# Four edits to a two-layer decoder kernel: kept output blocks in another order, half-width products beside each other, a second queue for weights, one O two steps later

## The chip, the cores and the metric

The kernel runs on one NeuronCore of a Trainium2 chip. A core has five engines that work side by side, each with a queue of its own that it goes through in order: TensorE (PE in the profile, with its weight loads as PEld), VectorE (DVE), ScalarE (ACT), GpSimd (POOL) and SyncE (SP). SyncE issues most of the transfers between device memory and the on-chip memory SBUF; GpSimd issues some. TensorE writes to a small memory, PSUM, in banks of 512 float32 columns. The metric is the device time of one execution in microseconds (us).

## The reference

Two residual layers over 1024 tokens of width 1024, then a last RMS norm.

```python
def reference(x, ...):
    for i in range(DEPTH):                       # DEPTH = 2
        h = rms_norm(x, norm_g[i])
        if i % N_MIXERS == 0:
            x = x + lru_mixer(h, ...)            # gated linear recurrence, width 1536
        else:
            x = x + fox_mixer(h, ...)            # 16 heads of 64, causal, with forget gates
    return rms_norm(x, final_g)

def fox_mixer(h, w_in, b_f, w_out):
    u = h @ w_in                                 # q, k, v, gate, f_logit
    cum = jnp.cumsum(jax.nn.log_sigmoid(f_logit + b_f), axis=1)
    logits = q @ k.T * scale + (cum_q - cum_k)   # causal mask
    o = softmax(logits) @ v
    y = o * jax.nn.silu(gate)
    return y @ w_out
```

## The kernel before

**Numbers in two parts.** Nearly all products are made three times: each float32 operand is split into a high part (`to_hi`, a rounding copy) and a low part (`to_lo`, what is left), and TensorE adds high x high, low x high and high x low (`gemm_steps`). Weights come from device memory in pieces of 128 x 512 (`split_weights`, `weights`, lines 111 to 126): `fetch` (line 56) issues the load on the queue that `loads_by` names, SyncE's; `wf` is the landing buffer (3 of them), `wh` and `wl` the two parts (4 each); ScalarE makes the high part, VectorE or GpSimd the low one.

**Stages.** Tokens are two halves of 512. First the recurrent layer (lines 184 to 531, up to about 440 us of the profile): for each of 12 blocks `product`, `conv`, `gates`, `silu`, `recur`, `outputs`, and `project_out` for pairs of blocks. `square_x` and `norm_row` make the first norm: eight squared blocks a half, seven of which are added into one tile, then two products with ones. The last square of each half lies in the fourth of four slots (`sq[3]`), which the other half's squares use too. `softplus` prepares the decay constants with small instructions. At the end of that layer x is stored to device memory (`x1d`), and `squares` and `inv_rms` make the next norm out of column sums: for every 128 tokens one product of a tile of sums with a column of ones, and one more for the last square, which is kept apart (`wait`, line 520).

Then the attention layer (lines 538 to 1127). Of a head `hd` of 16:

- `maxima(hd, c)` (line 762) goes through the four 128-row tiles of a half `c`: scores `S` in PSUM (two buffers), row maximum on VectorE, exponential on ScalarE, division by the sum (line 799 splits off the high part on ScalarE, line 800 the low part on VectorE, both float16 in `both`), and a transposing transfer on SyncE's queue into `turned_` (tile name pT).
- `weigh(hd, c)` (line 808) makes `O`: for each of 4 (first half) or 8 (second half) blocks `j` of keys, v's high and low columns (64 + 64) times the high and the low part of the turned weights, so 8 or 16 products into one PSUM bank. ScalarE (line 829) and VectorE (line 830) add the two 64-row halves of the bank into `yo`. `gated` (line 833) multiplies by the gate `sgs[pair]` after the second head of a pair.
- `kq_units`, `g_units`, `values` project the keys, queries, gates and values of later heads. `values(g)` serves four heads; it is made at the heads 3, 7 and 11 for the next four, from weights in four pieces (k = 0, 2, 4, 6), of which two are loaded before the run below, and the rest after it.

**Order.** `run(order, ...)` (line 853) takes a string: a digit takes the next step of that generator, a point the next step of `fill`, which is 6 products of other work. In a head `first` runs `weigh(hd, 0)` and `maxima(hd, 1)`, `second` runs `weigh(hd, 1)` and `maxima(hd + 1, 0)`; the strings are in lines 29 to 32 (`LAST` from head 12). TensorE's order is held by `tc.issue_after(pe[0].ins)`, which queues what is traced in its block behind the named instruction on the same engine, without waiting for it to end. Where nothing pins it, the order on each engine comes from a scheduler that runs when the program is built.

**The last heads.** From head 12 the fill is the output projection over the first six pairs of heads: `partial` (line 912) makes 16 blocks (8 blocks `db` of 128 outputs, both halves) of 18 products each. A block's x is fetched from `x1d` by GpSimd's queue, the product is added to it on VectorE (line 924), and it is stored again by GpSimd (line 926). It goes through a ring `R` of two buffers, except for four blocks of the first half that are kept in SBUF at a `home` (line 902): block 3 in a tile with the tag `sg`, shared with the gates `sgs` of the last pairs, and 5, 6 and 7 in a tile with the tag `T0`, the keys of the even heads. At the end `turned` (line 957) transposes the sums, adds the last two pairs' product and scales; `residual` (line 932) fetches the first half's other four blocks (0, 1, 2, 4) again.

## Time and profile before

| what | us |
|---|---|
| median of 3 runs (1078.75 to 1080.11) | 1079.31 |
| the profiled execution | 1079.6 |
| its span, first to last instruction | 1077.8 |
| TensorE busy | 1048.0 |
| VectorE busy | 782.1 |
| ScalarE busy | 621.6 |
| GpSimd busy | 113.2 |

The profile is of one execution. A row of the timeline has the start and the length in us, the engine, the line, the operation, and the tiles that it writes and reads; what stands in brackets is how long the engine had been idle, and what ended that. The line is that of the helper that issues the instruction (L60 for nearly all products), so one tells them apart by their tiles: `ops` for blocks of `partial`, `gps` for the projections, `vps` for values, `S` and `O` as above, `fps` for the transposes of the forget gates. Rows that end a wait by VectorE's name may stand for a transfer or another instruction of the same release; the time then tells which.

### The profile page before, as it was taken

Reading aid. Unit: us, or ns where it says so; the run is one execution under the profiler, and the core shown is the slowest. Engines: PE = TensorE matmul, PEld = TensorE weight load, DVE = VectorE, ACT = ScalarE, POOL = GpSimd, SP = SyncE. Lnnn points to the kernel's source line nnn. Section 1 sums busy time; section 2 is a strip of 40 time slices with the busy share of each in tenths; the row PEclk is TensorE's granted clock in tenths of the full one; section 3 lists DMA queues with packets and bytes.
Section 4 is the critical chain, followed back from the end, with each engine's and each line's share of the span. In section 5 each row is a group of like instructions: output and inputs, shape, how many; then the busy total and the mean of one; then the engine's idle time right before and its main releaser. Section 6 shows DMA issues by size and latency. Waiting matters only on the chain. (4 is left out here: it accounts for less than half of the span.)

```text
span 1077.8 us, 14962 instructions
## 1 busy us (share of the span) xinstructions
PE 1048.0 (97%) x5100; PEld 843.7 (78%) x5100; DVE 782.1 (73%) x1444; ACT 621.6 (58%) x1082; POOL 113.2 (11%) x91
## 2 busy tenths in 40 slices
PE   9999999999999999999999999999999999997997
PEld 7788888888888887797777797767977779765776
DVE  7889657766776589947878848788488866774665
ACT  8488453655465564745757636566466655653454
POOL 1322021202220210030000000000000000011200
PEclk9999999999999999999999999999999999998999
DMA  7111211222122112535878957899578885988994
GB/s 251 60 43 50 64 59 54 64 69 64 54 70 68 49 54 69 158 94 134 157 174 192 176 135 155 179 190 191 139 153 188 174 191 131 226 210 225 224 193 157
DMA packets 218508, 142.55 MB, mean 132 GB/s; under 512 B 161792, under 2 KB 178688, under 8 KB 218432
## 3 DMA queue, kind: packets, MB, share of 16 engines
q1 hardware_dynamic: 216032, 133.74, 52.3%
q0 software_dynamic: 2400, 7.87, 2.4%
q8 instruction: 40, 0.66, 0.3%
q14 instruction: 36, 0.29, 0.1%
HBM read 63.82 MB, written 14.81 MB: 73 GB/s over the span
## 5 line engine op out<-in xcount | busy, mean ns | idle before, releaser
L60 PE MATMUL gps<-hh,wh 128*128 128x512 f32 x576 | 227.3, 395 | 0.0
L60 PE MATMUL gps<-hh,wl 128*128 128x512 f32 x576 | 226.4, 393 | 0.8 <-DVE wl L101 0.7
L60 PE MATMUL gps<-hl,wh 128*128 128x512 f32 x576 | 226.6, 393 | 0.0
L90 ACT CAST wh<-wf 128x512 fp32r<-128x512 f32 (+2 forms) x162 | 97.3, 605 | 113.5 <-PE ops L60 43.0
L791 ACT ACTIVATE p<-S,m 128x128 f32<-128x128 f32 (+7 forms) x128 | 94.7, 740 | 67.6 <-DVE m L786 37.9
L101 POOL TENSOR_TENSOR wl<-wf,wh 128x512 fp32r<-128x512 f32 (+1 forms) x50 | 91.9, 1850 | 369.9 <-ACT wh L90 358.3
L60 PEld LDWEIGHTS gps<-hl,wh 128*128 128x128 f32 x576 | 108.4, 188 | 25.0 <-issue 0.5
L60 PEld LDWEIGHTS gps<-hh,wl 128*128 128x128 f32 x576 | 108.6, 189 | 22.5 <-DVE wl L101 1.0
L60 PEld LDWEIGHTS gps<-hh,wh 128*128 128x128 f32 x576 | 108.5, 188 | 21.6
L800 DVE SCALAR_TENSOR_TENSOR pp<-p,sums,pp 128x128 f16<-128x128 f32 (+7 forms) x128 | 103.1, 814 | 19.1 <-ACT pp L92 17.9
L92 ACT ACTIVATE pp<-p,sums 128x128 f16<-128x128 f32 (+7 forms) x128 | 95.5, 770 | 31.2 <-DVE sums L798 15.6
L786 DVE CUSTOM_DVE_ANT_0 S<-S,mask 128x128 f32<-128x128 f32 (+7 forms) x128 | 97.2, 760 | 16.9 <-PE S L60 15.6
L60 PE MATMUL S<-T,U 96*128 96x512 f32 (+7 forms) x384 | 94.3, 355 | 8.1 <-ACT p L791 8.0
L101 DVE TENSOR_TENSOR wl<-wf,wh 128x512 fp32r<-128x512 f32 x112 | 74.4, 668 | 25.8 <-ACT wh L90 25.6
L60 PEld LDWEIGHTS S<-T,U 128*128 128x128 f32 (+1 forms) x384 | 67.9, 190 | 26.2 <-ACT p L791 14.3
L389 DVE TENSOR_TENSOR x<-x,ops 128x512 f32<-128x512 f32 x80 | 54.1, 683 | 41.5 <-PE ops L60 41.4
L60 PE MATMUL ups<-hh,wh 128*128 128x512 f32 x192 | 75.6, 395 | 1.2 <-ACT hh L92 1.2
L60 PE MATMUL ups<-hl,wh 128*128 128x512 f32 x192 | 76.6, 399 | 0.2
L60 PE MATMUL ops<-yh,wl 128*128 128x512 f32 x192 | 75.7, 394 | 0.9 <-DVE wl L101 0.9
L60 PE MATMUL ops<-yh,wh 128*128 128x512 f32 x192 | 75.8, 396 | 0.5 <-DVE x L513 0.5
L60 PE MATMUL ups<-hh,wl 128*128 128x512 f32 x192 | 75.8, 395 | 0.0
L60 PE MATMUL O<-pT,v 128*128 128x512 f16 (+3 forms) x396 | 71.3, 322 | 3.8 <-DMA pT<-pp 3.6
(188 smaller groups left out, 1985.8 us busy)
## 6 DMA issues: line engine op xcount, KB each, us to landing
wf<-in_w SPq DMA_DIRECT2D x106, 256.0 KB
wf<-in_wo SPq DMA_DIRECT2D x64, 128.0 KB
T<-qkh SPq DMA_DIRECT2D x64, 128.0 KB
U<-qkh SPq DMA_DIRECT2D x64, 128.0 KB
x<-in_xt SPq DMA_DIRECT2D x16, 256.0 KB
wvf<-in_wv SPq DMA_DIRECT2D x32, 128.0 KB
x1d<-x SPq DMA_DIRECT2D x16, 256.0 KB
wf<-in_wv SPq DMA_DIRECT2D x16, 256.0 KB
```

Of the source, the lines that this page charges most:

```text
L60: pe[0] = nc.tensor.matmul(*args, **kw)
L90: nc.scalar.copy(hi, src)
L92: nc.scalar.activation(hi, src, AF.Copy, scale=scale)
L101: return eng.tensor_tensor(lo, src, f32(hi), ALU.subtract)
L389: nc.vector.tensor_tensor(x, x, pt, ALU.add)
L786: nc.vector.tensor_tensor_reduce(S[:, :n], S[:, :n], mask[:, SEQ - n :], -1.0, -NEG, ALU.add, ALU.min, accum_out=m)
L791: seen[0] = nc.scalar.activation(p, S[:, :n], AF.Exp, bias=m, scale=-1.0, accum_out=sums[:, i : i + 1])
L800: nc.vector.scalar_tensor_tensor(both[:, :, 1], p, r, both[:, :, 0], ALU.mult, ALU.subtract)
```

## The change

Four edits, and small ones with them.

- **Kept blocks.** The blocks of the first half that stay in SBUF are 4, 5, 6, 7 instead of 3, 5, 6, 7. Block 4 is the one in the tile with the tag `sg`, whose other half is later block 3's; the tile `T0` holds 2, 5, 6, 7. `residual` fetches 0 to 3 again.
- **Low products.** In `weigh(hd, 1)` over a whole half, the low part of the turned weights meets v's high columns alone (the product low x low is left out). Each such product has 64 columns of the array, and writes rows 0 to 63 or 64 to 127 of the bank; they follow in pairs, one for each half of the array. The steps that `run` sees stay four.
- **Values' last weights.** At heads 3, 7 and 11 the pieces k = 4 and 6 are loaded by GpSimd's queue, and are issued before the last maxima tile of `second` instead of after the run. O's copies on ScalarE (line 829) are queued behind the last of those casts, and in every head but the last, for the second half, behind the last split of line 799.
- **Head 14's last O.** `second` of head 14 has its first O two points later.
- In the first norm the last square has a slot of its own, the square roots go behind the squares of both halves, and `softplus` behind the taps of `conv(0)`. In the second, the second half's last square is added on VectorE like the others.

```diff
     pe = [None]
     loads_by = [nc.sync]
+    loaded_last, cast_last = [None], [None]
     def fetch(to, src):
-        loads_by[0].dma_start(to, src)
+        loaded_last[0] = loads_by[0].dma_start(to, src)
     def matmul(*args, **kw):
...
         if eng is nc.scalar:
             if scale is None:
-                nc.scalar.copy(hi, src)
+                cast_last[0] = nc.scalar.copy(hi, src)
             else:
                 nc.scalar.activation(hi, src, AF.Copy, scale=scale)
...
         acc = long("m2")
         sq = [z[:, cs] for z in (long("th"), long("ti")) for cs in halves]
+        sq_ = long("sg")
+
+        squared = [None]
         def square_x(h):
...
             sums[h].append(to)
             for k in range(KT):
-                z = sq[k % 4] if k else to
-                nc.scalar.activation(z, xs[h][k], AF.Square)
+                z = sq_[:, halves[h]] if k == KT - 1 else sq[k % 4] if k else to
+                squared[0] = nc.scalar.activation(z, xs[h][k], AF.Square)
                 if k == KT - 1:
                     sums[h].append(z)
...
             row = ps.tile([P, HALF], F32, tag="O", name="rsrow")
-            for i, sq_ in enumerate(sums[h]):
-                matmul(row, onesf, sq_, start=i == 0, stop=i == len(sums[h]) - 1)
+            for i, z in enumerate(sums[h]):
+                matmul(row, onesf, z, start=i == 0, stop=i == len(sums[h]) - 1)
             r_ = rs[:, halves[h]]
-            nc.scalar.activation(r_, row, AF.Sqrt, bias=epst, scale=1.0 / SEQ)
-            return nc.vector.reciprocal(r_, r_)
+            with tc.issue_after(squared[0].ins):
+                nc.scalar.activation(r_, row, AF.Sqrt, bias=epst, scale=1.0 / SEQ)
+            nc.vector.reciprocal(r_, r_)
         for _ in zip(split_x(0), square_x(0)):
...
                 for _ in zip(split_x(1), square_x(1)):
                     pass
-                done = norm_row(0)
+                norm_row(0)
             else:
                 gates(n - 1)
...
                 product(gps[:, 1], 1, first[1])
                 norm_row(1)
-                with tc.issue_after(done.ins):
+            conv(n, both)
+            if n == 0:
+                with tc.issue_after(state[0]["tap"].ins):
                     softplus()
-            conv(n, both)
             if n % 2 and n > 1:
                 fill = itertools.chain(fill, project_out((n - 3) // 2))
...
                         x,
                         lambda: nrm.tile([P, HALF], F32, tag="sq" if db else "ss", name="sq", bufs=2),
-                        wait=db == KT - 1,
+                        wait=h == 0 and db == KT - 1,
                     )
             rms_row(sums, rs1[h], rms1[h])
...
                 if ex:
                     src.append((wf[:, k : k + 2], slice(256, 256 + ex)))
+                loads_by[0] = nc.gpsimd if k > 3 and not ex else nc.sync
                 parts += split_weights(src, (2, 256 + ex), nc.scalar, nc.gpsimd if ex else nc.vector)
-                if k == 2:
+                loads_by[0] = nc.sync
+                if k == 2 or k == 6 and not ex:
                     yield
             Vs[2 * g], Vs[2 * g + 1] = [], []
...
         stats, pT = {}, {}
+        split_last = [None]
+
+        def after(i):
+            return tc.issue_after(behind[i].ins) if behind else nullcontext()
+
         def maxima(hd, c):
...
                 nc.vector.tensor_scalar(r, r, 1.0 / TOP, None, ALU.mult)
                 nc.vector.reciprocal(r, r)
-                to_hi(both[:, :, 0], p, nc.scalar, scale=r)
+                split_last[0] = nc.scalar.activation(both[:, :, 0], p, AF.Copy, scale=r)
                 nc.vector.scalar_tensor_tensor(both[:, :, 1], p, r, both[:, :, 0], ALU.mult, ALU.subtract)
                 turns.append(
...
             O = ps.tile([P, HALF], F32, tag="O", name="O")[:, : end - begin]
             nj = end // P
+            beside = c == 1 and sub.stop - sub.start == HALF
             for j in range(nj):
                 v = V[j][:, 2 * s : 2 * s + 2].rearrange("p a d -> p (a d)")
                 q = max(begin, j * P)
-                for t in range(2):
+                for t in range(1 if beside else 2):
                     p = turned_[:, j, t, q - c * HALF : end - c * HALF]
-                    matmul(O[:, q - begin :], v, p, start=j == t == 0, stop=j == nj - 1 and t == 1)
-                if j % 2 and j < nj - 1:
+                    matmul(O[:, q - begin :], v, p, start=j == t == 0, stop=not beside and j == nj - 1 and t == 1)
+                if j % 2 and j < nj - 1 and (j % 4 == 3 or not beside):
                     yield
+            if beside:
+                yield
+                for j, a in ((0, 0), (1, 1), (2, 0), (3, 1), (4, 0), (5, 1), (6, 1), (7, 0)):
+                    q = max(begin, j * P)
+                    matmul(
+                        O[a * HD : (a + 1) * HD, q - begin :],
+                        V[j][:, 3 * s],
+                        turned_[:, j, 1, q - c * HALF : end - c * HALF],
+                        start=False,
+                        stop=j > 5,
+                    )
+                    if j == 3:
+                        yield
             r0, r1 = s * HD, (1 - s) * HD
             to, one = yo[r0 : r0 + HD], unit_v[:, hd // 4 : hd // 4 + 1]
-            nc.scalar.activation(to, O[r1 : r1 + HD], AF.Copy, scale=one[r1 : r1 + HD])
+            with after(1), tc.issue_after(split_last[0].ins) if c and hd < HEADS - 1 else nullcontext():
+                nc.scalar.activation(to, O[r1 : r1 + HD], AF.Copy, scale=one[r1 : r1 + HD])
             nc.vector.scalar_tensor_tensor(to, O[r0 : r0 + HD], one[r0 : r0 + HD], to, ALU.mult, ALU.add)
             yield
...
         seen = [None]
-        def run(order, *gens, fill=iter(()), side=iter(())):
-
-            for i in order:
+        behind = []
+
+        def run(order, *gens, fill=iter(()), side=iter(()), vals=None):
+
+            for n, i in enumerate(order):
+                if vals and n == order.rfind("1"):
+                    next(vals)
+                    behind[:] = loaded_last[0], cast_last[0]
                 with tc.issue_after(pe[0].ins):
                     next(fill if i == "." else gens[int(i)], None)
...
         def home(db):
-            if db == 3:
+            if db == 4:
                 two = at.tile([P, 2, HALF], F32, tag="sg", name="x3")
-                homes[3], homes[2] = two[:, 0], two[:, 1]
+                homes[4], homes[3] = two[:, 0], two[:, 1]
             elif db == 5:
                 four = tu.tile([P, 4, HALF], F32, tag="T0", name="x4")
-                homes.update((4 + i, four[:, i]) for i in range(4))
+                homes.update(zip((2, 5, 6, 7), (four[:, i] for i in range(4))))
             return homes[db]
...
                     split_out(db + 1)
-                kept = c == 0 and db in (3, 5, 6, 7)
+                kept = c == 0 and db > 3
                 x = home(db) if kept else rpool.tile([P, HALF], F32, tag="R", name="xp")
                 nc.gpsimd.dma_start(x, x1d[c, :, db])
...
                 two = tu.tile([P, 2, HALF], F32, tag="U0", name="x0")
                 homes[0], homes[1] = two[:, 0], two[:, 1]
-                for d in (0, 1, 2, 4):
+                for d in range(4):
                     fetch(homes[d], x1d[c, :, d])
             if c == 0:
...
                 fill = chain(g_units(pair + 1), kq_units(pair + 2, ((1, (0,)),)))
             first, second = LAST if hd > 11 else ORDER
+            if hd == HEADS - 2:
+                second = "1.1..1..1....0.0.00"
             if hd == HEADS - 1:
                 first = "1..1.0.1.0.1..."
...
             if hd == 14:
                 side = chain(side, late())
+            vals = None
             if hd % 4 == 3 and hd < 12:
-
                 vals = values(hd // 4 + 1)
                 next(vals)
-            run(second, weigh(hd, 1), maxima(hd + 1, 0), fill=fill, side=side)
+            run(second, weigh(hd, 1), maxima(hd + 1, 0), fill=fill, side=side, vals=vals)
+            behind.clear()
             drain(side)
             gated(hd, 1)
...
             if hd < 12:
                 drain(fill)
-            if hd % 4 == 3 and hd < 12:
+            if vals:
                 drain(vals)
         quarters = [slice(0, 256), slice(256, HALF)]
         gated(15, 0)
```

2 lines of the change are left out of this document (1 added, 1 removed).

## The prediction

> **What bounds the kernel now.** I read first the page's busy times, then the stages, then TensorE's waits.
>
> ```profile
> PE 1048.0 (97%) x5100; PEld 843.7 (78%) x5100; DVE 782.1 (73%) x1444; ACT 621.6 (58%) x1082; POOL 113.2 (11%) x91
> ...
> 0.00:440.00 440.00, 436.09 (x1872) 351.97 (x1873) 328.45 (x373) 256.74 (x369) 86.58 (x52) 1.00 0.23 73
> 440.00:506.00 66.00, 65.28 (x390) 57.29 (x389) 45.53 (x98) 37.86 (x66) 10.32 (x9) 1.00 0.46 125
> 506.00:930.00 424.00, 413.67 (x2203) 332.94 (x2202) 315.11 (x772) 254.05 (x499) 0.00 (x0) 1.00 0.79 168
> 930.00:1000.00 70.00, 62.57 (x272) 46.75 (x271) 45.84 (x99) 34.61 (x64) 10.92 (x20) 0.95 0.92 233
> 1000.00:1040.00 40.00, 39.20 (x189) 29.97 (x189) 27.29 (x64) 19.54 (x37) 4.91 (x10) 1.00 1.05 218
> 1040.00:1077.80 37.80, 31.16 (x184) 24.82 (x182) 19.90 (x43) 18.81 (x49) 0.51 (x1) 0.96 0.50 160
> ...
> PE S L60 <- ACT p L791: 8.0, 9, 2.1
> PE ops L60 <- DVE sums L797: 5.5, 1, 5.5
> PE O L60 <- DMA pT<-pp: 3.6, 5, 1.4
> ```
>
> The stage rows give start and end, length, then the busy time of PE, PEld, DVE, ACT and POOL, PE's granted clock, the share of the DMA engines and GB/s. TensorE is busy 97% of the span and at full clock everywhere but in 930 to 1000, where 7.4 us of 70 are idle and the clock falls to 0.95, and in the tail after 1040, which the change does not touch. So a change pays in two ways: fewer columns through TensorE, or less idle time in that one stage. Over the rest of the heads' part (506 to 930) DVE has work for 315 of 424 us and ACT for 254, so neither has to become the bound when TensorE is a few per cent quicker. The first 440 us hold 4 us of idle time in all: nothing that is moved there can win more.
>
> **The order of kept blocks.** The 5.5 us wait is one event, at 985 us. First VectorE's queue, then GpSimd's, then TensorE's, then two pieces of the chain:
>
> ```profile
> 984.40 0.69 DVE L839 TENSOR_TENSOR yo<-yo,sg 128x512 f32<-128x512 f32 x1
> ...
> 986.31 0.89 DVE L800 SCALAR_TENSOR_TENSOR pp<-p,sums,pp 128x640 f16<-128x640 f32 x1
> 990.13 0.69 DVE L924 TENSOR_TENSOR x<-x,ops 128x512 f32<-128x512 f32 x1 [2.93 <-DMA x<-x1d]
> ...
> 974.54 0.54 POOL L921 DMA_DIRECT2D xp<-x1d  x1 [3.56 <-DMA x1d<-xp]
> ...
> 981.32 0.54 POOL L921 DMA_DIRECT2D xp<-x1d  x1 [4.13 <-DMA x1d<-xp]
> 985.38 0.54 POOL L921 DMA_DIRECT2D x<-x1d  x1 [3.53 <-DVE sums L798]
> 992.37 0.55 POOL L926 DMA_DIRECT2D x1d<-xp  x1 [6.45 <-DVE sums L798]
> ...
> 984.27 1.08 PE L60 MATMUL S<-T,U 128*128 128x512 f32 x4 [0.31 <-ACT p L791]
> 990.87 0.80 PE L60 MATMUL ops<-yhh,wh 128*128 128x512 f32 x1 [5.52 <-DVE sums L797]
> 991.47 0.63 PE L60 MATMUL ops<-yhh,wl 128*128 128x512 f32 x1
> ...
> 990.89 5.46 PE ops L60 x12
> ...
> 997.28 2.79 PE ops L60 x12
> ```
>
> GpSimd's load of x at 985.38 is that of kept block 3 of the first half: its home has the tag sg, and it is free only when gated(13, 1) has read the gate at 984.40 to 985.09 (the name "sums" on the row is of a later instruction). The data land at about 990.1, the add of line 924 waits until then at the head of VectorE's queue, the PSUM buffer that it empties stays full, and TensorE, two products further, waits for that buffer. After 5.5 us of idleness the next 12 products take 5.46 us where 12 take 2.79 later on: 2.67 more, the clock of 0.95 above. The event costs 5.5 + 2.7 = **8.2 us**.
>
> After the change block 3 of the first half goes through the ring R like its neighbours, and block 4 is the first with a home. The ring's load that GpSimd issued at 974.54 was for the product after block 3's; that slot now serves block 3, which is multiplied at that moment. Block 4's load still waits for gated(13, 1), so it is issued at 985.4 and lands at 990.1. But its product is the one that TensorE starts at 985, right after the S of 984.27, and 18 products at 0.23 us (12 in 2.79) with a few S products between them end near 990. The add is then late by up to 1 us, and that stays inside the two PSUM buffers. Behind that load in GpSimd's queue stand the store of block 3 and the loads of the ring: 4 us or so per trip (3.53 to 4.13 in the rows), against two products of about 5 us each. The number of loads and stores is the same, and at the end blocks 0 to 3 are fetched by SyncE instead of 0, 1, 2 and 4: four transfers either way, beside the last products. Gain between 0 (the next load late by as much) and 8.2; I take **7.2**, one us for block 4's add.
>
> **Low products side by side.** For each head but the last, the second half's weigh runs 16 products: eight pairs with all 128 columns of v's high and low part, once on the high and once on the low part of the turned weights.
>
> ```profile
> 876.42 2.83 PE O L60 x16
> ...
> L60 PE MATMUL O<-pT,v 128*128 128x512 f16 x182 | 45.7, 381 | 3.8 <-DMA pT<-pp 3.6
> ...
> 476.08 0.38 PE L64 MATMUL fps<-ident,fz 128*16 128x128 f32 x2
> ...
> 491.86 0.39 PE L60 MATMUL gps<-hh,wh 128*128 128x512 f32 x1
> 492.08 0.27 PE L64 MATMUL fps<-ident,fz 128*16 128x128 f32 x1
> 492.11 0.48 PE L60 MATMUL gps<-hh,wh 128*128 128x512 f32 x1
> 492.43 0.40 PE L60 MATMUL gps<-hh,wl 128*128 128x512 f32 x1
> 492.66 0.39 PE L60 MATMUL gps<-hl,wh 128*128 128x512 f32 x1
> ```
>
> Sixteen products take 2.83 us, and the low ones are half of them: 1.41 us for 5 x 512 + 384 + 256 + 128 = 3328 columns. The change gives each of them 64 of the 128 columns of the array, four to the lower and four to the upper half. The lower half gets 512 + 512 + 512 + 128 = 1664 columns, the upper 512 + 512 + 384 + 256 = 1664. If the halves run at the same time, the low part takes half, and a head saves **0.71 us**; for 15 heads 10.6. If they run one after the other, it saves nothing. No row here has two products at once, so this is the upper bound and zero the middle one. What else the change adds is two changes of shape per block of low products: 17 blocks (heads 0 to 11 one each, 12 and 13 two, 14 one, as the strings of the orders put them), 34 changes. The nearest row is the transpose at 492.08 that uses 16 columns. From its start to the second full product after it pass 0.35 us; a full product strides 0.23, and a transpose strides 0.11 (the pair at 476.08: 0.38 less the 0.27 of one), so the two changes cost 0.01.
>
> [...]
>
> How much of the 0.71 arrives? The rows of waits list 9 waits for S and 5 for the turned weights. With 33 weighings and 32 rounds of maxima in the heads, 14 of 65 stages, 22%, hold such a wait, and what is won ahead of one is lost in it. Elsewhere TensorE goes on with fill. So I take three quarters, 0.53 us per head, 15 x 0.53 = **8.0 us**. The lower bound is below zero; its price stands with the rivals.
>
> **Norms.** In the layer's second norm the last square of the second half is now added by VectorE, which takes away 4 of the 8 column sums:
>
> ```profile
> 461.00:466.00 5.00, 1.90 (x16) 1.96 (x16) 0.26 (x1) 1.00 0.59 182
> ...
> L175 DVE TENSOR_TENSOR sq<-sq x12: 679/684/1254, 427.5 to 457.0; 128x512 f32<-128x512 f32 x12
> ```
>
> The 16 records of the second half (two per sum) keep TensorE 1.90 us, half of it 0.95. The added sum costs VectorE 0.68 us on the way to the norm, but values' products stand between the column sums and run on. Between 0 and 0.95; I take **0.5**. The first layer's norm: its first row is no longer queued behind the other half's squares, the root goes behind those squares on ScalarE, and softplus's 2 ScalarE and some 20 VectorE instructions go behind the taps of conv(0). TensorE covers all of it with the products of block 1 (436 busy of 440), so nothing; with that cover gone it could cost the stage's whole idle time over again at most, 3.9 us.
>
> **Head 14's last O.**
>
> ```profile
> 1014.47 1.04 PE L60 MATMUL O<-pT,v 128*128 128x512 f16 x4 [0.80 <-DMA pT<-pp]
> ...
> 879.25 22.78 PE vps L60 x192
> ...
> L829 ACT ACTIVATE yo<-O,unit_v x33: 468/685/688, 527.6 to 1057.0; 64x512 f32<-64x512 f32 x31, 64x256 f32<-64x256 f32 x2
> ```
>
> It starts 0.80 us late, for a transposed block. Two steps of fill, 12 products or 2.8 us, now go ahead of it, so the **0.8** goes; what it feeds (yo of pair 7) is needed only a head later.
>
> **Values' weights and the O copies.** At heads 3, 7 and 11 the loads of the last four k move from SyncE to GpSimd, whose queue is empty from 506 to 930 (0.00 above), two loads each, and are issued before the last maxima tile. Their casts come no earlier than the buffers wh and wl that fill still reads. Already now the values' 192 products run in 22.78 us, 0.119 each, without a gap, so there is nothing to win: 0. O's copy on ScalarE (0.685 us) goes behind the last split of the next head's first round, and at those three heads behind the last cast. Behind it are exponentials of the next round; TensorE has 2.1 us of O and the rest of fill meanwhile, so 0 too. If the casts are late, all that stands behind them on ScalarE is late by one wait for S of the longest kind, 2.1 us, three times: -6 at worst.
>
> **Sum.** 7.2 + 8.0 + 0.5 + 0.8 = 16.5 us. The profiled execution took 1079.6 us (span 1077.8 and 1.8 around it), which gives 1063.1. It lies 0.3 above the median of the three runs, so against that 1062.8: **1063**.
>
> **Rivals.**
> (a) The halves of the array don't overlap: the low products keep their 1.41 us. Then 1079.3 - 8.5 = 1071. For it: no row shows two products at once. Against it: the narrow transpose starts at once and holds up nothing.
> (b) The stall of 985 us moves instead of going: block 4's load waits for the same release, the load lands after 4.7 us, and the DMA engines have a share of 0.92 to 1.05 in that part, so that with TensorE 8 us sooner the transfers come late in their turn. For it: those shares. Against it: of TensorE's waits for a transfer the list has only the 3.6 us for pT, and block 4 has two products' time more than block 3. The 7.2 are lost: 1079.3 - 9.3 = 1070.
> (c) Slower: products of half the array don't stream, each begins when the one before it has ended. A product of 512 columns lasts 0.381 us by itself against the 0.216 by which the four of an O follow each other (1.04 less 0.39, by 3). Eight of them, each 0.165 over its stride (the shorter ones taken alike), cost 8 x 0.165 = 1.3 us per head, 19.8 for 15 heads. With the other terms 1079.3 - 8.5 + 19.8 = 1091. It decides as soon as one low product takes over 0.07 us more than now (8.5 / 120). Against it: again the transpose's rows.
> (d) Both (a) and (b), and the values' casts late: about 1078, no change that can be told.
>
> **Numbers.** Forecast 0.60, (a) 0.16, (b) 0.12, (c) 0.08, (d) 0.04. What can be told from no change is 0.2%, 2.2 us. So faster 0.88, same 0.04, slower 0.08. The low end is everything at its upper bound: 1079.3 - 8.2 - 10.6 - 0.95 - 0.8 = 1058.8, and two more for waits for S and turned weights that go of themselves: 1057. The high end takes in (a) and (b) and most of (d) with some of the values' loss: 1077. (c) stays outside.
>
> **What would show it.** The kernel's row "PE ops <- DVE sums" of 5.5 us should be gone, 930 to 1000 should have a clock of 1.00, and GpSimd's first load of a kept block should still wait for the gate of pair 6. A second half's O should take 2.1 to 2.3 us for 16 products; 2.8 says (a), over 3.5 says (c). The waits for S and turned weights may grow by 2 us together. Wrong would be: a new wait of ops between 985 and 1010 (b), a gap before vps at heads 3, 7 and 11, or O's of a second half that take 2.1 us while the heads' part is no shorter.

## The result, and the profile after

The changed kernel takes 1080.04 us (median of 12 runs, 1076.47 to 1082.83), the kernel before on the same chip 1079.56 us. The ratio is 0.9996, with a 95% interval of 0.9981 to 1.0011: no difference. The profiled execution took 1079.7 us, its span is 1077.9. The prediction said 1063 us.

First the busy times of the changed kernel, its stages (length; busy time of PE, PEld, DVE, ACT, POOL; PE's clock; share of the DMA engines; GB/s), and TensorE's longest waits (sum, number, longest):

```profile
PE 1044.7 (97%) x5092; PEld 839.4 (78%) x5092; DVE 786.5 (73%) x1445; ACT 621.5 (58%) x1082; POOL 112.0 (10%) x97
...
0.00:440.00 440.00, 434.92 (x1862) 350.27 (x1863) 328.00 (x370) 255.25 (x366) 82.21 (x52) 1.00 0.23 73
506.00:930.00 424.00, 408.88 (x2189) 328.63 (x2188) 314.24 (x765) 251.51 (x495) 3.38 (x6) 0.99 0.78 166
930.00:1000.00 70.00, 68.71 (x319) 51.66 (x318) 50.44 (x112) 38.67 (x71) 11.83 (x22) 1.00 0.96 240
1000.00:1040.00 40.00, 35.14 (x158) 26.40 (x157) 25.34 (x58) 18.26 (x35) 3.78 (x7) 0.96 1.00 221
...
PE S L61 <- ACT p L804: 12.8, 8, 3.0
PE O L61 <- DMA pT<-pp: 5.5, 5, 1.7
PE ops L61 <- DVE xp L957: 1.4, 1, 1.4
```

The stage of 930 to 1000 has become what was wanted: TensorE is busy for 68.7 of 70 us where it had 62.6, at full clock, and the 5.5 us wait is gone. But idle time has come up in two other places. In 506 to 930 TensorE is busy for 408.9 us instead of 413.7, and the waits of S for the exponential have grown from 8.0 to 12.8 us. They grow at the heads with values: at 3, 7 and 11 together S waits 2.3 us for it before and 7.2 us after (1.7, 2.5 and 3.0). In 1000 to 1040 it is busy for 35.1 instead of 39.2 us, and now that stage has the clock of 0.96.

Lined up product by product, the two traces give a ledger. Each number is the start of the same product after minus before, in us, taken from the rows of TensorE; the second column is what the stretch added.

```
end of stretch                               offset   added
first product of values (461 us)             +2.3    +2.3   first layer and its norm
start of the heads' rounds (514 us)          +1.4    -0.9   second norm
heads 0 to 2                                 +1.5    +0.1
head 3 with values                           +2.8    +1.3
heads 4 to 6                                 +1.8    -1.0
head 7 with values                           +3.8    +2.0
heads 8 to 10                                +2.7    -1.1
head 11 with values                          +4.6    +1.9
heads 12 and 13                              +3.7    -0.9
past the event at 985 us                     -5.1    -8.8
fill at 1026 us                              -1.3    +3.8
last product of the kept blocks (1038 us)    +0.5    +1.8
```

Such a ledger has noise. Six kernels of the runs below change nothing ahead of 930 us. There they stand at -0.6 to -1.9: -0.2 to +0.4 at 461 us, then -0.5 to -1.1 in the three heads with values together and -0.7 to -1.6 in the other heads. So single entries of a us or two in the heads are not read, only what several runs show alike. Three things stand out: the event was worth even more than forecast; 5.6 of its 8.8 us are given back, nearly all of it between 1006 and 1029 us (times of the kernel before); and the three heads with values cost 5.2 us together, while the other heads win 2.9, of which up to 1.6 is noise.

The event first. VectorE's last read of the gate, GpSimd's loads of kept blocks in the changed kernel:

```profile
987.33 0.68 DVE L867 TENSOR_TENSOR yo<-yo,sg 128x512 f32<-128x512 f32 x1
...
988.31 0.54 POOL L954 DMA_DIRECT2D x<-x1d  x1
...
993.54 1.59 POOL L954 DMA_DIRECT2D x<-x1d  x3
```

Block 4's load still comes only behind the gate's last read (987.33 + 0.68 = 988.01), as the prediction had it, and no product waits for it. What comes next is in the same kernel's rows of SyncE's queue, ScalarE and TensorE:

```profile
999.50 2.06 SPq L58 DMA_DIRECT2D x<-x1d  x3
1001.66 9.12 SPq L815 DMA_TRANSPOSE pT<-pp  x2
...
1015.29 0.62 ACT L91 CAST woh<-wf 128x512 fp32r<-128x512 f32 x1 [6.16 <-DMA wf<-in_wo]
...
1003.93 0.62 PE L61 MATMUL S<-T,U 128*128 128x384 f32 x2 [1.75 <-ACT p L804]
1019.19 0.50 PE L61 MATMUL ops<-yhh,wh 128*128 128x512 f32 x1 [1.40 <-DVE xp L957]
```

Two transposing transfers, of 14 and 16 blocks, keep SyncE's queue for 9.1 us. Behind them stands the load of the last output weights, whose cast ScalarE has at the head of its queue for 6.2 us. TensorE then waits in small pieces: 1.75 and 1.40 us in these rows, and 1.71 us for a turned block ahead of an O at 1029 us.

The low products did what they should. The rows of one second half's O give its first and last start. In the kernel before:

```profile
L60 PE MATMUL O<-pT,v x16: 219/379/390, 539.0 to 541.8; 128*128 128x512 f16 x10, 128*128 128x384 f16 x2, 128*128 128x256 f16 x2, 128*128 128x128 f16 x2
...
539.03 2.99 PE L60 MATMUL O<-pT,v 128*128 128x512 f16 x16
541.83 0.47 PE L60 MATMUL gps<-hl,wh 128*128 128x512 f32 x1
```

In the changed kernel, where half of the products have 64 columns of the array:

```profile
L61 PE MATMUL O<-pT,v x16: 219/379/404, 540.5 to 542.7; 128*128 128x512 f16 x5, 128*64 128x512 f16 x5, 128*128 128x384 f16 x1, 128*128 128x256 f16 x1
...
540.47 2.41 PE L61 MATMUL O<-pT,v 128*128 128x512 f16 x16
542.80 0.50 PE L61 MATMUL gps<-hl,wh 128*128 128x512 f32 x1
```

16 products start within 2.2 us instead of 2.8, and over the 12 heads that have such a group of 16 the last start comes 0.59 us sooner. The halves of the array do work at the same time: in three of the four pairs the two low products start 0.002 to 0.004 us apart. But the product that follows the group comes only 0.46 us sooner (2.33 us after the first start instead of 2.80). The rest goes at the two changes of shape. The last product of full width, with 128 columns, is followed after 0.15 us, where one of that size was followed after 0.06 before; the last of the group is followed after 0.15 us instead of 0.03. That is 0.22 us per group, where the prediction had 0.01.

Last, head 7, one of the three with values: SyncE's load of a weight of the fill, its cast on ScalarE, and TensorE. The kernel before:

```profile
738.46 0.59 SPq L57 DMA_DIRECT2D wf<-in_w  x1
741.50 0.62 ACT L90 CAST wh<-wf 128x512 fp32r<-128x512 f32 x1 [1.35 <-DMA wf<-in_w]
```

The changed kernel, with GpSimd's load of a value weight:

```profile
739.79 0.54 POOL L58 DMA_DIRECT2D wf<-in_wv  x1 [12.71 <-DVE wl L102]
741.39 0.60 SPq L58 DMA_DIRECT2D wf<-in_w  x1
745.66 0.62 ACT L91 CAST wh<-wf 128x512 fp32r<-128x512 f32 x1 [3.71 <-DMA wf<-in_w]
746.79 0.73 PE L61 MATMUL S<-T,U 128*128 128x512 f32 x2 [2.50 <-ACT p L804]
```

Before, the cast follows its load's issue by 3.0 us and ScalarE was idle for 1.35. After, it follows by 4.3 us, with GpSimd's load of a value weight running, and ScalarE was idle for 3.71. The exponential stands behind the cast, and S behind the exponential: 2.5 us of TensorE.

### The profile page after: what moved, and what is told of

Same layout as the page of the kernel before. It is cut to its first block, busy times and chain, and to the rows that moved or that the text cites. A ratio compares the mean times of both kernels' runs of the same rounds, so it can differ in the third digit from the quotient of the medians.

```text
span 1077.9 us, 14961 instructions
## 1 busy us (share of the span) xinstructions
PE 1044.7 (97%) x5092; PEld 839.4 (78%) x5092; DVE 786.5 (73%) x1445; ACT 621.5 (58%) x1082; POOL 112.0 (10%) x97
## 5 line engine op out<-in xcount | busy, mean ns | idle before, releaser
L102 POOL TENSOR_TENSOR wl<-wf,wh 128x512 fp32r<-128x512 f32 (+1 forms) x50 | 87.5, 1760 | 376.7 <-ACT wh L91 376.6
L812 ACT ACTIVATE pp<-p,sums 128x128 f16<-128x128 f32 (+7 forms) x128 | 95.4, 771 | 30.5 <-DVE sums L811 10.9
L61 PE MATMUL S<-T,U 96*128 96x512 f32 (+7 forms) x384 | 95.1, 357 | 13.1 <-ACT p L804 12.8
L799 DVE CUSTOM_DVE_ANT_0 S<-S,mask 128x128 f32<-128x128 f32 (+7 forms) x128 | 97.1, 759 | 11.3 <-PE S L61 10.4
L61 PE MATMUL ops<-yl,wh 128*128 128x512 f32 x192 | 74.6, 395 | 0.2 <-DVE yl L102 0.2
```

The costliest lines, as they stand in the source:

```text
L61: pe[0] = nc.tensor.matmul(*args, **kw)
L102: return eng.tensor_tensor(lo, src, f32(hi), ALU.subtract)
L799: nc.vector.tensor_tensor_reduce(S[:, :n], S[:, :n], mask[:, SEQ - n :], -1.0, -NEG, ALU.add, ALU.min, accum_out=m)
L812: split_last[0] = nc.scalar.activation(both[:, :, 0], p, AF.Copy, scale=r)
```

## The experiments

Each run is timed in rounds beside the kernel before, whose median was between 1079.1 and 1079.9 us. Ratios are to that, with their 95% intervals.

**One part at a time.** The low products side by side alone (the change to `weigh` without the order of its copies):

```diff
+            beside = c == 1 and sub.stop - sub.start == HALF
-                for t in range(2):
+                for t in range(1 if beside else 2):
...
+                    matmul(
+                        O[a * HD : (a + 1) * HD, q - begin :],
+                        V[j][:, 3 * s],
```

> The kernel before with the low products side by side alone. Theory P (each edit pays what it pays at its own place; other edits lose as much): the second halves' O shorten by 0.56 to 0.6 us a head, as in the trace of the change, and most of it arrives: 6 to 8 us less. Theory S (what TensorE wins in the heads is lost again in waits for S and for the turned weights, whichever edit wins it): less than 3 us less, and the waits for S and pT grow from 11.6 us to 16 or more.

The order of kept blocks alone:

```diff
-            if db == 3:
+            if db == 4:
...
-                kept = c == 0 and db in (3, 5, 6, 7)
+                kept = c == 0 and db > 3
```

> The kernel before with the blocks 4 to 7 kept alone. Theory P: the wait of 5.5 us at 985 and the slow clock after it go, 8 us or a little more less at the start of the product after block 3, and 7 to 8 us less at the end. Theory D (the transfers of the last part bound it: SyncE's queue stands behind transposing transfers, weights and x come late): the 8 us are won at 990 but more than half is lost by 1038, with waits for S, ops or O of 1 to 2 us each; at the end 1 to 4 us less.

The values' weights and the order of O's copies alone:

```diff
+                loads_by[0] = nc.gpsimd if k > 3 and not ex else nc.sync
...
+                if vals and n == order.rfind("1"):
+                    next(vals)
+                    behind[:] = loaded_last[0], cast_last[0]
```

> The kernel before with the values' last weights on GpSimd's queue, their earlier issue, and the order of O's copies on ScalarE, and nothing else. Theory P: this is where the heads lose: 4 to 6 us more, by waits for S of 2 to 3 us at the heads 3, 7 and 11, where ScalarE's queue stands behind a cast of weights. Theory S: within 1 us of before, since no engine is quicker.

Both norms alone:

```diff
+            with tc.issue_after(squared[0].ins):
+                nc.scalar.activation(r_, row, AF.Sqrt, bias=epst, scale=1.0 / SEQ)
...
-                        wait=db == KT - 1,
+                        wait=h == 0 and db == KT - 1,
```

> The kernel before with the edits of the two norms and of softplus alone. Theory P: the first 440 us are 2 to 2.5 us longer, as in the trace of the change, and the second norm gives 0.9 back: 1 to 2 us more. My prediction had 0.5 less. Theory R (the offset before 440 us is a chance of that one execution): no difference at 440 us.

Measured: side by side 1093.67 us, ratio 1.0126 [1.0094, 1.0158]; kept order 1077.24, 0.9971 [0.9953, 0.9990]; values 1085.28, 1.0056 [1.0033, 1.0079]; norms 1081.02, 1.0006 [0.9986, 1.0025]. Worked out from the medians, the four are +13.9, -2.6, +5.5 and +1.2 us: 18 us slower in sum, where all together are no slower. So the parts don't add. Side by side neither of its theories came; the kept order came as theory D, the values as theory P. The norms' interval includes no change, but the trace decides: at 461 us it stands at +1.6, where the 17 other changed kernels here that keep the first norm as it was stand at -0.2 to +0.6.

The side by side products alone lose at heads 3, 7 and 11. TensorE's waits, and a row of SyncE's queue and one of ScalarE at head 3, in that run:

```profile
PE vps L60 <- ACT wh L90: 13.8, 3, 5.5
...
628.67 0.43 SPq L57 DMA_DIRECT2D wf<-in_wv  x1
633.45 0.62 ACT L90 CAST wh<-wf 128x512 fp32r<-128x512 f32 x1 [9.57 <-DMA wf<-in_wv]
```

In the kernel before one row stands for both of the last loads:

```profile
610.21 0.92 SPq L57 DMA_DIRECT2D wf<-in_wv  x2
```

The scheduler that orders the built program has put the last load of value weights far back in SyncE's queue, behind pieces of T and U and transposes; the cast is 9.6 us late, and values' products wait 13.8 us in three places. In the kernel before both loads stand ahead of those transposes, and there is no such wait. Whether the scheduler moved the load because the products are shorter or because they are traced in another order was not tried. So the values' edit has a purpose that its own cost hides: it issues these loads early.

**The pair, and its two halves.** Side by side and values together; then the same with the value weights on SyncE's queue, still issued early; then the same as the first without the order of O's copies behind the last split:

> The low products side by side and the whole edit of values' weights, on the kernel before. Theory V (the side by side products are paid for at the heads 3, 7 and 11: the kernel build puts the last load of the values' weights late into SyncE's queue, and GpSimd's queue only shortens that loss): 0.46 us won at each other head, 1 to 2 us lost at each of the three, no wait of values for a cast; 0 to 3 us more than before. Theory A (effects add: 13.9 + 5.5): 19 us more.

```diff
-                loads_by[0] = nc.gpsimd if k > 3 and not ex else nc.sync
```

> As the pair of side by side products and values' edit, but all of the values' weights loaded by SyncE's queue, still issued before the last maxima tile. Theory Q (the queue is what counts): the last load stands behind pieces and transposing transfers again, and values wait for casts: 3 to 7 us at each of the heads 3, 7 and 11, 9 to 15 us more than the pair. Theory E (the earlier issue is what counts): within 2 us of the pair.

```diff
-            with after(1), tc.issue_after(split_last[0].ins) if c and hd < HEADS - 1 else nullcontext():
+            with after(1):
```

> As the pair, but O's copies on ScalarE are no longer queued behind the last split of the next head's first round. Theory C (that order costs time at every head, as it holds back yo and what SyncE sends of it): 2 us or more less than the pair. Theory N (no one waits for yo): within 1 us of the pair.

Measured: 1083.65 us, 1.0025 [1.0003, 1.0048]; 1077.56, 0.9978 [0.9958, 0.9997]; 1080.61, 0.9998 [0.9977, 1.0020]. The pair came 3.9 us slower than the kernel before, a little over the 0 to 3 of theory V and far from A. The queue is worth 6.1 us, in a direction that neither theory had expected: SyncE's, the fuller one, is the better. The early issue is what repairs side by side, not GpSimd's queue. The waits of S in the pair:

```profile
PE S L61 <- ACT p L799: 11.3, 7, 2.9
```

And in the pair with SyncE's queue:

```profile
PE S L61 <- ACT p L798: 6.9, 8, 1.6
```

At the heads 3, 7 and 11 S waits 7.9 us in the pair and 2.4 us with SyncE's queue, 5.4 us less. The order of O's copies makes 3.0 us between the medians; the interval overlaps with that of the pair, so it stays open.

**Other loads moved as well.** The changed kernel with the first layer's norm as before, and with the projections' weights of pairs 1 to 6 and the first step of pair 7 on GpSimd's queue:

```diff
+                    loads_by[0] = nc.gpsimd if 0 < pair < 7 or pair == 7 and hs == (0,) else nc.sync
                     kqw[is_k] = list(weights(w1[is_k * 8 + pair], lo_eng=low(pair)))
+                    loads_by[0] = nc.sync
...
+                loads_by[0] = nc.gpsimd if 0 < pair < 7 else nc.sync
                 gw[0] = list(weights(w1[16 + pair], lo_eng=low(pair)))
+                loads_by[0] = nc.sync
```

> The change without its edit of the first norm, and with the weights of the keys', queries' and gates' projections of the pairs 1 to 7 (7 for its first step alone) on GpSimd's queue too. Theory Q (the waits for S at the heads 3, 7 and 11 come from a weights' load that stands behind pieces and transposing transfers in SyncE's queue): those three waits of 1.7 to 3.0 us go or fall under 0.5, and the time is 1069 to 1073. Theory L (the transfers themselves are slow there, whichever queue issues them): the waits stay, 1077 to 1080.

Measured: 1067.18 us (five executions), 0.9876 [0.9844, 0.9907]. It beats both kernels, by 12.6 us at the medians, and lies under the 1069 to 1073 that theory Q had forecast. As that theory said, the three waits are gone: in its trace S doesn't wait for the exponential at the heads 3, 7 and 11. Which of the moved loads wins the time was not tried one by one.

**Taking the two suspects out of the changed kernel.** First both, the first layer's norm as before and the value weights on SyncE's queue; beside it the norm alone:

> The changed kernel with two parts undone: the first layer's norm as before (its root, its squares' buffer and softplus's place), and the values' last four weights on SyncE's queue again, still issued ahead of the last maxima tile. Theory Q2 (what swallowed the gain are these two parts: 2.4 us in the first 440 us, and some 6 us of late casts at heads 3, 7 and 11, as the pair with the loads on SyncE was 6.1 us quicker than the pair with them on GpSimd): 1080.0 - 2.4 - 6.1 = 1071.5, between 1069 and 1074; the waits of S for the exponential fall from 12.8 us to 8 or less. Rival R (the effects do not add: TensorE sooner at heads 3, 7 and 11 finds the casts just as late whatever queue loads them): 1076 to 1080, the waits of S stay over 11 us.

> The changed kernel with the first layer's norm as before, all else as changed. It tells the two parts of the run beside it apart. Theory N (the first 440 us give back 2.4 us, and that passes to the end): 1077.6, between 1076.5 and 1078.7. Rival (a shift of the start is taken up by waits later on): 1079.5 to 1080.5.

Measured: 1073.15 us, 0.9944 [0.9921, 0.9966], and 1078.03 us, 0.9983 [0.9968, 0.9999]. The norm gives back 2.0 us at the medians. By the intervals alone that can't be told from the changed kernel; the first product of values says it better, at +2.3 us in the changed kernel and at 0.0 and +0.2 in these two. The queue gives 4.9 us more, and the intervals of the two runs don't overlap. Both times came as theories Q2 and N said. The waits of S fell to 10.4 us in all, not to 8, but 4.0 of that is one wait in head 14, at 998 us. At the heads 3, 7 and 11 S waits 2.0, 2.5 and 2.5 us with GpSimd's queue, and 0.3, 0.7 and 1.4 us with SyncE's: 4.6 us less. Head 7 with the value weights on SyncE's queue:

```profile
734.77 0.59 SPq L58 DMA_DIRECT2D wf<-in_w  x1
735.41 0.43 SPq L58 DMA_DIRECT2D wf<-in_wv  x1
737.68 0.62 ACT L91 CAST wh<-wf 128x512 fp32r<-128x512 f32 x1 [1.91 <-DMA wf<-in_w]
738.81 0.73 PE L61 MATMUL S<-T,U 128*128 128x512 f32 x2 [0.73 <-ACT p L798]
```

And on GpSimd's:

```profile
736.89 0.54 POOL L58 DMA_DIRECT2D wf<-in_wv  x1 [12.71 <-DVE wl L102]
738.18 0.59 SPq L58 DMA_DIRECT2D wf<-in_w  x1
742.76 0.62 ACT L91 CAST wh<-wf 128x512 fp32r<-128x512 f32 x1 [3.71 <-DMA wf<-in_w]
743.90 0.73 PE L61 MATMUL S<-T,U 128*128 128x512 f32 x2 [2.54 <-ACT p L799]
```

The same cast, the same exponential behind it: 1.91 us of idle time against 3.71, and 0.73 us of TensorE against 2.54. In the ledgers of the two runs heads 3, 7 and 11 add 0.4 us together on SyncE's queue and 5.2 us on GpSimd's. That agrees with the 4.9 us between the medians.

On SyncE's queue the projection's weight goes first, the value weight stands behind it, and the cast follows the issue by 2.9 us; with two queues GpSimd's value weight was asked for 1.3 us before it, and the cast follows by 4.6 us. What goes with the delay is in the packets of the same place in the kernel before and in the changed kernel, where the cast follows by 3.0 and 4.3 us. In the kernel before, from 738.5 to 741 us, all packets are of SyncE's queue and keep the DMA engines busy with a share of 0.92. In the changed kernel, from 741.4 to 743.9 us, GpSimd's packets have a share of 0.34 and SyncE's 0.62; from 741.5 to 742 us it is 0.96 and 0.03.

**Where the event's gain goes.** The kept order alone wins 6.8 us at the event and has 2.6 us at the end. Its wait of O and its transposes:

```profile
PE O L60 <- DMA pT<-pp: 6.0, 6, 3.7
...
994.04 1.33 SPq L57 DMA_DIRECT2D x<-x1d  x3
995.46 10.87 SPq L802 DMA_TRANSPOSE pT<-pp  x2
```

The first suspect were the fetches right ahead of the transposes. They were put behind them, in the kept order and in the best version:

```diff
+                with tc.issue_after(turns[-9].ins):
+                    for d in range(4):
+                        fetch(homes[d], x1d[c, :, d])
```

> The kernel before with the other order of kept blocks alone, and SyncE's four fetches of blocks 0 to 3 issued behind the four transposing transfers of head 15's first half, so that the transposes of 14 and 16 blocks have no fetch right ahead of them. Theory D (these two transposes take 5.2 and 5.6 us because the x transfers run with them, and that gives back what the event at 985 us had won): they take 2 to 3 us each, the wait of O for pT of 3.7 us near 1004 goes, and the time is 1077.2 - 3.7 = 1073.5, between 1072 and 1075. Rival L (transposes of this size take that long by themselves, or wait for the other queues' traffic): 5 us each as before, 1076 to 1078. Rival B (the fetches are now late for the first turned block): a new wait of TensorE for x near 1025, over 1078.

> The kernel of 1067.2 us (changed kernel with the first layer's norm as before and the projection weights of pairs 1 to 7 on GpSimd's queue) with the same four fetches behind the transposes of head 15. Its transposes of 14 and 16 blocks took 5.5 and 3.6 us behind the fetches, its O waited 3.0 us for pT. Theory D: 1067.2 - 3 = 1064.2, between 1062.5 and 1066. Rivals L and B: 1066.5 to 1070.

Measured: 1075.57 us, 0.9964 [0.9948, 0.9980], and 1067.49 us, 0.9888 [0.9861, 0.9914]: neither can be told from the run without it, and only the second lies in the range of a theory (L and B). The pinned run of the kept order, SyncE's queue and the wait:

```profile
992.44 11.96 SPq L802 DMA_TRANSPOSE pT<-pp  x2
...
PE O L60 <- DMA pT<-pp: 7.2, 6, 4.7
```

No fetch stands ahead, and the two transposes keep the queue for 12.0 us instead of 10.9; the wait is longer. That theory fell.

The second suspect were GpSimd's three loads, with a control on the kernel before:

```diff
+                if kept and db > 4:
+                    nc.gpsimd.memset(x, 0.0)
+                else:
+                    nc.gpsimd.dma_start(x, x1d[c, :, db])
```

> The other order of kept blocks alone, and GpSimd's loads of x for blocks 5, 6 and 7 of the first half left out (the homes are filled with zeros instead, so the output lacks x there). Theory C (rival b of the prediction in another place: these three loads of 256 KB are issued together at 994.5 to 996.1, and with the loads and stores of the ring beside them they slow the transposing transfers of 14 and 16 blocks, 5.2 and 5.6 us; that gives back what the event at 985 us had won): the two transposes take 2.0 to 3.2 us each, as their medians over the heads are 2.45 and 2.94, the 3.7 us wait of O for pT goes, and the time is 1077.2 - 4 = 1073, between 1071.5 and 1074.5. Rival L (the transposes are slow there for another reason): one of them stays over 4.5 us, the wait stays over 2.5 us, 1075.5 to 1078.

> The kernel before, its order of kept blocks unchanged, with the same three loads left out. It tells what the loads cost by themselves. Theory C: the transpose of 16 blocks falls from 6.8 to 3 us, but TensorE waited only 0.8 us for it, since the event at 985 us had kept it back: 1079.9 - 0.8 = 1079.1, between 1078 and 1080. If the loads cost time in another way, this run is as much faster as the one beside it: under 1077.

Measured: 1075.09 us, 0.9960 [0.9944, 0.9977], and 1077.61 us, 0.9975 [0.9960, 0.9991]. The kept order without the loads, its waits, its transposes and ScalarE:

```profile
PE ops L60 <- DVE x L927: 3.1, 1, 3.1
PE O L60 <- DMA pT<-pp: 2.9, 7, 0.9
...
995.04 7.05 SPq L802 DMA_TRANSPOSE pT<-pp  x2
...
1006.60 0.62 ACT L90 CAST woh<-wf 128x512 fp32r<-128x512 f32 x1 [5.94 <-DMA wf<-in_wo]
```

The transposes are quicker, 7.1 us instead of 10.9 for both, and the long wait for pT is gone. But TensorE now waits 3.1 us for VectorE's add, which stands behind the split of a weight that ScalarE casts 5.9 us late. The time is 2.1 us under that of the kept order alone (their intervals overlap), and the control, which has its event still, is 1.9 us under the kernel before. So these loads cost about as much in either order; they are not what takes the gain. They do slow the transposes, which take 3.8 us less together without them. But at the end theory C's times did not come: the kept order lies above its range, the control below.

The third suspect was the queue of those last weights:

```diff
+                    loads_by[0] = nc.gpsimd
                     for d in range(2):
                         fetch(wt[:, 2 * d : 2 * d + 2], wo1[half * 4 + b * 2 + d, :, 6:8])
+                    loads_by[0] = nc.sync
```

> The other order of kept blocks alone, with the last output weights (the tiles woh and wol that head 14's second half loads) on GpSimd's queue instead of SyncE's. Theory S (the gain of the event at 985 us is given back because the cast of those weights stands at the head of ScalarE's queue, idle 4.2 and 3.6 us in the kernel with the kept order alone, 5.2 us in the kernel before, for loads that SyncE can issue only behind the transposes of 14 and 16 blocks): ScalarE's idle time ahead of a cast of woh falls below 1.5 us and the time to 1077.2 - 3.5 = 1073.7, between 1072 and 1075.5. Rival M (the DMA engines are full between 990 and 1005 us, share 0.94 to 1.2, so it does not matter which queue asks): idle times of over 3 us stay, ahead of the cast or of a split, and the time is 1076 to 1079.

> The kernel before with the same last output weights on GpSimd's queue, its order of kept blocks unchanged. Theory S: the event at 985 us keeps TensorE back anyway, so little is won: 1078 to 1079.5. Rival M: 1079 to 1081. Under S the kept order then wins more beside it than the 2.6 us that it won alone.

> The kernel of 1067.2 us with the same last output weights on GpSimd's queue. Theory S: 1067.2 - 3 = 1064, between 1062 and 1066. Rival M: 1066.5 to 1069.5.

Measured: kept order 1079.83 us, 1.0008 [0.9991, 1.0025]; kernel before 1078.43, 0.9990 [0.9972, 1.0009]; best version 1069.65, 0.9906 [0.9875, 0.9937]. Nothing is won. In the kept order the idle time has only changed its place; ScalarE, the stages of 5 us there, and TensorE's wait:

```profile
1012.45 0.72 ACT L92 ACTIVATE pp<-p,sums 128x512 f16<-128x512 f32 x1 [5.39 <-DMA pT<-pp]
...
1005.00:1010.00 5.00, 0.54 (x3) 0.21 (x2) 2.76 (x8) 1.28 (x3) 0.55 (x1) 1.00 1.21 132
1010.00:1015.00 5.00, 2.61 (x7) 1.51 (x7) 0.75 (x1) 1.02 (x2) 0.00 (x0) 0.51 1.10 316
...
PE O L60 <- DMA pT<-pp: 9.3, 8, 6.8
```

The weights come in time and the transposes late. The DMA engines have a share of 1.1 to 1.2 there (as the profile counts it, which gives 1.33 at one place of the kernel before), and what was taken out of one queue left another transfer late. That fits rival M, which speaks of full engines, but the times bear it out only in part: the kept order came above its range, the best version 0.15 us above it, and the kernel before in the range of theory S. The nearest to a run with emptier engines is the one without GpSimd's loads: from 1000 to 1010 us the share is 0.86 there instead of 1.09 in the kept order, and the transposes are quicker, but the cast of the last weights was late all the same.

**The best version with the value weights on SyncE's queue:**

> The kernel of 1067.2 us with the values' last four weights on SyncE's queue again, still issued early; the projection weights stay on GpSimd's. Theory Q2 (a load of GpSimd's at heads 3, 7 and 11 reaches the cast later than one of SyncE's; the changed kernel without the first norm's edit won 4.9 us by it): some of it is won already, as GpSimd's other loads took their place on SyncE's queue, so 1067.2 - 2 = 1065, between 1063 and 1066.5. Rival W (with SyncE's queue relieved of the projection weights the values' queue no longer matters): 1066.5 to 1069.

Measured: 1069.99 us, 0.9908 [0.9885, 0.9931], against 1067.18 [0.9844, 0.9907] with them on GpSimd's. The forecast of a gain was wrong; the intervals overlap, so the other sign isn't shown either. With the projections' weights on GpSimd's queue it no longer pays to have the values' on SyncE's: here too S doesn't wait for the exponential at the heads 3, 7 and 11, though the two kinds of weights are on two queues.

## Why the prediction was wrong, point by point

**The step that failed first is the price of nothing for the values' weights and the O copies**: "Already now the values' 192 products run in 22.78 us, 0.119 each, without a gap, so there is nothing to win: 0". There was nothing to win, but there was 4.9 us to lose (with and without GpSimd's queue in the changed kernel with the first norm as before; 6.1 in the pair). The prediction looked at the products that use these weights. The loss is elsewhere: at the three heads a projection's weight, loaded on SyncE's queue at the same time, arrives later, its cast stands ahead of the exponential on ScalarE, and S waits. The bound that the prediction kept, 2.1 us three times, was the right wait and nearly the right size (7.2 us at the three heads in the changed kernel), but was given a chance only as part of rival (d). The late cast was that of a projection, not one of the values'.

**Low products, -8.0 forecast.** The mechanism was right, but the two changes of shape, put at 0.01 us, cost 0.22: of a possible 0.71 us only 0.46 reach the next product, against 0.53 forecast. Over 12 heads that is 5.5 us, and only 2.7 of them stand at 930 us in the best form without other edits (the pair on SyncE's queue), of which 0.6 to 1.9 also stand in kernels without the edit; 2.2 are left at its end. Where the rest goes is not shown stretch by stretch. "Elsewhere TensorE goes on with fill" was too hopeful, and the side effect was not thought of: this edit changes the order in which the scheduler lays the loads, and the part alone is 13.9 us slower.

**Kept blocks, -7.2 forecast.** On the spot it is 8.8 us, more than the upper bound of 8.2, and the new order does what was said, block by block. But the 7.2 were taken to the end of the kernel, and they don't get there: 5.6 us come back by 1029 us in the changed kernel, and the part alone is worth 2.6 us. Rival (b) had the condition right, DMA engines with a share of 0.92 to 1.05, but it placed the new stall at block 4's load. The waits came at the transposes and the last weights; what causes them stays open, as three suspects were taken out one by one and none gave the gain back.

**Norms, -0.5 forecast.** The second norm won 0.9. The first layer's part was priced at nothing, for TensorE's cover; it is 2.3 us slower in the trace, 1.6 us in that of the norms alone, and taking it out of the changed kernel brings 2.0 at the medians. That is within the 3.9 named as the price without cover; which instruction lost the cover was not tried.

**Head 14's last O, -0.8 forecast.** Not tried by itself. At its place the 0.8 us wait is gone, in the changed kernel and in both runs that take suspects out of it. The waits of O for pT in the whole changed kernel grew from 3.6 to 5.5 us, with 1.7 of them at 1029 us; those two runs have the same edit and no such wait there, so this edit alone doesn't make it.

**Rivals.** (a) fell: the halves overlap. (c) fell with it. (d) named the time that came, but by another way: it needed (a).

**The sum.** The terms of the event and of head 14 were about right at their places, and that of the low products somewhat too large. What failed is that they were carried to the end and added. From the changed kernel to 1063 us 17 us are missing. By the ledger and the medians they are 4.9 for the queue, 5.1 in the heads (8.0 less 2.9), 4.8 from the event on (7.2 and head 14's 0.8, less the 8.8 - 5.6 that stay) and 1.9 for the norms (+2.3 - 0.9 where -0.5 stood): 16.7. The queue and the first norm are shown by taking them out; the other two sums are only read from one execution each.

What fills the DMA engines from 995 to 1015 us in the changed kernel can be read from its packets: those of 256 bytes, which are the transposes' (128 for each block, 147456 in the whole kernel), have a share of 0.54, GpSimd's queue 0.33, and SyncE's other loads 0.24. What stays open is how they could be thinned out, whether that would keep the event's gain, and how much of the 12.6 us of the best version is owed to each load that it moves.

## What to carry to other kernels

Of the 8.8 us that the event gave, 5.6 came back in the stage behind it: before adding a gain to the sum, read that stage, and where the DMA engines have a share near 1 there, as here (1.05 from 1000 to 1040 us in the kernel before), allow for the gain being lost again. The load that was moved to an idle queue still took its part of the DMA engines, 0.34 with SyncE's packets at 0.62 beside it, where those had 0.92 before: look at which cast stands at the head of a queue at that moment (here ScalarE was idle for 3.71 us ahead of it instead of 1.91), not only at those who use the moved data. And where a scheduler lays the order, an edit to the products of one engine can change every queue; compare the order of the loads before pricing it.

## What the runs showed of the hardware

Two groups of products on the two halves of the array's columns ran at the same time: in three of the four pairs the two start 0.002 to 0.004 us apart, where products of 512 columns at full width follow each other by 0.216. Each change between full and half width cost about 0.1 us: 0.09 into the group (0.15 instead of 0.06 to the next product) and 0.12 out of it (0.15 instead of 0.03). Of the possible 0.71 us per head 0.46 are left. What the array does at such a change no run shows.

In the kernel before the DMA engines are full around 1005 us, mostly with packets of transposing transfers, while few bytes move: SyncE's two transposes, a stage of 5 us there, and the packets of SyncE's queue (q1) and of GpSimd's (q0) from 1000 to 1010 us, with their number, MB and share:

```profile
999.65 10.86 SPq L802 DMA_TRANSPOSE pT<-pp  x2
...
1005.00:1010.00 5.00, 5.00 (x24) 4.17 (x24) 4.17 (x15) 2.64 (x9) 0.54 (x1) 1.00 1.33 121
q1 hardware_dynamic: 2185, 0.78, 75.2%
q0 software_dynamic: 297, 0.98, 38.6%
```

The stage has a share of 1.33 at 121 GB/s. In the 10 us SyncE's queue issues nothing but the two transposes; its packets of 256 bytes take 0.65 of the engines for 52 GB/s, and GpSimd's of 4 KB 0.38 for 98 GB/s. Over all heads a transpose of 16 blocks keeps the queue for 2.93 us (median); here it is 6.8. At head 7, from 743.5 to 746 us of the same trace, nearly all packets are the transposes' (2692 of 2724): a share of 1.26 for 276 GB/s. So 52 GB/s for 0.65 is what they moved beside GpSimd's packets, not what they move alone.
